# Convolution input projection by Strassen's seven products, on normed input, with the second layer's memory keys computed first

## The chip, the cores and the metric

One core of a Trainium2 chip runs the whole program. The metric is device time in microseconds, the median of several executions; the profile is of one execution. Five engines work from queues of their own: TensorE (PE; its weight loads are listed as PEld), VectorE (DVE), ScalarE (ACT), GpSimd (POOL) and SyncE (SP), which here issues the transfers between DRAM and the on-chip memory SBUF. TensorE writes its sums into PSUM, from which VectorE and ScalarE read. All data are float32.

## The reference

1024 tokens of 1024 features pass two layers. Layer 0 has windowed attention and retention side by side. Layer 1 is a gated convolution over the tokens. After each comes a cross-attention with four heads into 256 memory tokens, and at the end a norm. What the change touches is layer 1's convolution, and the keys of the cross-attention behind it:

```python
def conv_mixer(xn, w_in, conv_w, conv_b, w_out):
    s = xn.shape[1]
    gb, gc, u, gate = jnp.split(xn @ w_in, 4, axis=-1)
    z = gc * u
    zp = jnp.pad(z, ((0, 0), (C_CONV - 1, 0), (0, 0)))
    conv = conv_b
    for j in range(C_CONV):
        conv = conv + zp[:, j:j + s] * conv_w[j]
    y = gb * conv * jax.nn.silu(gate)
    return y @ w_out
```

Here `xn = rmsnorm(x, g)`: x times the gain g of its feature and times R, the inverse root of the token's mean square. `w_in` is 1024 x 4096. The keys are `memn @ wkv[:, :1024]`, 1024 features for 256 memory tokens.

## The kernel before

**Layout.** Activations lie with features on the 128 partitions and tokens along the row: eight tiles of 128 x 1024. A weight tile is 128 x 1024 too: for one output tile of 128 features, the eight 128 x 128 blocks of the contraction side by side.

**Precision.** A float32 number is split into a part `hi`, rounded to the type float32r, and the rest `lo`. A product takes three matmuls, hi hi + hi lo + lo hi (`mm3`, L125 to L130). ScalarE copies `hi`, VectorE subtracts to get `lo`: L64 and L65 for weights, L144 and L145 (`split`) for most others, L156 and L157 where a gain is applied on the way.

**Weights.** `Weights` streams weight tiles in a fixed order: a raw tile is loaded (L53, two buffers `wraw`), split into `whi` and `wlo` (three buffers each), and taken by a projection. When tile i is taken, tiles up to i + 2 are prepared.

**A projection.** `dense` (L132) computes 128 output features: for each half of the tokens, eight contraction tiles by three matmuls of 512 columns, 24 matmuls into one PSUM bank; then a function evacuates it.

**The convolution stage.** `out_proj` of layer 0's cross-attention adds the residual (L227), and squares and sums the features (L186, L188, L202). `gained` splits x times the gain of its feature (L156, L157). `norm` makes R from the sums, by two matmuls for each half of the tokens (L195, L196) and a chain on ScalarE and VectorE (L167 to L172). R isn't in the matmuls' input: evacuation multiplies by it (`scaled`, L214). `conv_in` (L478) takes eight groups of four weight tiles (gate, gb, gc, u), 32 calls of `dense`:

```python
            for done in (gate, gb, gc, u):
                self.dense(xs, done)
            if m < 5:
                next(kv)
```

`gate` and `gc` are scaled at evacuation and once more by R on GpSimd (L488, L495), since the other factor lacks its R; `gb` and `u` multiply PSUM by that (L491, L498). Three taps and the product with y1 follow (L504 to L509).

**The memory keys.** `mem_k` computes one tile of 128 key features at each step: 24 matmuls of 256 columns. Five steps stand behind the first five groups, three behind the last (`for _ in kv: pass`); then the convolution's outputs are split and projected by `out_proj`, with the memory values (`mem_v`) in between. The normed memory is kept in DRAM and loaded as four tiles `mn`.

**The order.** Buffers are named by tag, and each tag has a fixed number (L108: `xh`, `xl`, `r` 8 each, `T` and `t` 5, `e` and `v` 4); an instruction that writes a buffer waits until the readers of what was in it are done. A planner orders each engine's instructions ahead of time, by a simulated time line: earlier instructions of the program go first, but whatever its simulation finds ready may go in between. On the chip each engine follows that fixed order and waits by semaphores.

## Time and profile before

| | us |
|---|---|
| median of 3 runs (1514.28 to 1515.32) | 1514.37 |
| span of the profiled execution, first to last instruction | 1513.2 |
| TensorE busy in it | 1483.5 |
| VectorE, ScalarE, GpSimd busy | 769.1, 564.8, 230.3 |
| convolution projection: first evacuation of y to last of z | 799.3 to 1149.2 |
| layer 1's three last key tiles | 1148 to 1157 |

The profiled execution has no time of its own beside its span; the median of the runs is 1.2 us above it. In the profile's rows, `x16 | 11.0, 690` means 16 instructions, 11.0 us busy in all, 690 ns each on average. A row of a time line gives the start in us, the length in us, engine, source line, operation, output and inputs, shape, and the count where equal neighbours are merged; in brackets the idle time before it and what ended that. A row of one tile gives the shortest, median and longest instruction in ns, then the first and last start in us. Matmuls overlap, so their busy lengths are not to be added up.

### The profile page before, as it was taken

Reading aid. Unit: us, or ns where it says so; the run is one execution under the profiler, and the core shown is the slowest. Engines: PE = TensorE matmul, PEld = TensorE weight load, DVE = VectorE, ACT = ScalarE, POOL = GpSimd, SP = SyncE. Lnnn points to the kernel's source line nnn. Section 1 sums busy time; section 2 is a strip of 40 time slices with the busy share of each in tenths; the row PEclk is TensorE's granted clock in tenths of the full one; section 3 lists DMA queues with packets and bytes.
Section 4 is the critical chain, followed back from the end, with each engine's and each line's share of the span. In section 5 each row is a group of like instructions: output and inputs, shape, how many; then the busy total and the mean of one; then the engine's idle time right before and its main releaser. Section 6 shows DMA issues by size and latency. Waiting matters only on the chain.

```text
span 1513.2 us, 18550 instructions
## 1 busy us (share of the span) xinstructions
PE 1483.5 (98%) x7410; PEld 1256.1 (83%) x7410; DVE 769.1 (51%) x1143; ACT 564.8 (37%) x983; POOL 230.3 (15%) x157
## 2 busy tenths in 40 slices
PE   8999999999999999999999999999999999999996
PEld 6878888888788888888888888888888888888996
DVE  7656765556673356444354333332336336446555
ACT  6434652433463244343243111211115225334554
POOL 2300103233401210000211111111110120000233
PEclk9999999999999999999999999999999999999998
DMA  5410104121464521002522221111123532111464
GB/s 212 165 44 29 56 29 139 58 82 43 139 209 153 167 82 44 29 29 70 193 81 102 63 63 56 56 56 56 42 84 113 180 127 74 36 30 40 133 206 151
DMA packets 44421, 140.77 MB, mean 93 GB/s; under 512 B 5552, under 2 KB 11824, under 8 KB 44080
## 3 DMA queue, kind: packets, MB, share of 16 engines
q1 hardware_dynamic: 44336, 139.60, 28.3%
q8 instruction: 58, 0.95, 0.3%
q14 instruction: 27, 0.22, 0.0%
HBM read 112.32 MB, written 23.07 MB: 89 GB/s over the span
## 4 chain that ended last, share of the span: by engine, by line
PE 85%; DVE 5%; DMA 4%; POOL 2%; ACT 1%; issue 1%; SPq 1%; DVEq 0%; POOLq 0%; ACTq 0%
PE psd L130 23%; PE psd L128 23%; PE psd L129 23%; PE pssc L130 3%; PE pssc L129 3%; PE pssc L128 3%; PE psa L128 2%; PE psa L129 2%; PE psa L130 2%; PE psa L311 1%; DMA swap<-bk 1%; DMA swap<-bq 1%; PE psa L621 1%; POOL bk L346 1%; POOL bq L346 1%
## 5 line engine op out<-in xcount | busy, mean ns | idle before, releaser
L128 PE MATMUL psd<-xh,whi 128*128 128x512 f32 (+2 forms) x1736 | 662.0, 384 | 8.4 <-ACT whi L64 7.3
L129 PE MATMUL psd<-xl,whi 128*128 128x512 f32 (+2 forms) x1736 | 663.9, 383 | 0.0
L130 PE MATMUL psd<-xh,wlo 128*128 128x512 f32 (+2 forms) x1736 | 663.1, 383 | 0.0
L128 PEld LDWEIGHTS psd<-xh,whi 128*128 128x128 f32 x1736 | 326.2, 188 | 69.5 <-ACT whi L64 7.8
L129 PEld LDWEIGHTS psd<-xl,whi 128*128 128x128 f32 x1736 | 326.3, 188 | 59.5 <-DVE xl L157 0.3
L130 PEld LDWEIGHTS psd<-xh,wlo 128*128 128x128 f32 x1736 | 326.2, 188 | 59.5
L64 ACT CAST whi<-wraw 128x1024 fp32r<-128x1024 f32 (+1 forms) x155 | 162.0, 1046 | 428.1 <-PE psd L129 306.7
L65 DVE TENSOR_TENSOR wlo<-wraw,whi 128x1024 fp32r<-128x1024 f32 (+1 forms) x155 | 200.6, 1295 | 68.0 <-ACT whi L64 66.1
L188 POOL TENSOR_TENSOR ssq<-ssq,xold 128x512 f32<-128x512 f32 (+2 forms) x54 | 78.1, 1446 | 573.6 <-ACT xold L186 484.3
L227 DVE TENSOR_TENSOR xnew<-psd,xold 128x512 f32<-128x512 f32 x48 | 32.9, 690 | 147.2 <-PE psd L130 143.8
L186 ACT ACTIVATE xold<-xnew 128x512 f32<-128x512 f32 (+2 forms) x63 | 36.4, 580 | 89.2 <-DVE xnew L227 48.9
L144 ACT CAST Th<-psa 128x512 fp32r<-128x512 f32 (+1 forms) x62 | 34.2, 588 | 68.9 <-PE psa L311 36.8
L145 DVE TENSOR_TENSOR Tl<-psa,Th 128x512 fp32r<-128x512 f32 (+1 forms) x62 | 42.1, 686 | 28.3 <-ACT Th L144 28.3
L488 POOL TENSOR_TENSOR y<-y,R 128x512 f32<-128x512 f32 x16 | 24.2, 1514 | 185.4 <-ACT y L487 185.4
L214 DVE TENSOR_TENSOR q<-psd,R 128x512 f32<-128x512 f32 x32 | 22.1, 691 | 53.9 <-PE psd L130 53.8
L611 ACT ACTIVATE P<-pssc,mx 128x256 f32<-128x256 f32 x64 | 29.5, 473 | 43.2 <-DVE mx L609 43.2
L214 DVE TENSOR_TENSOR z<-psd,R 128x512 f32<-128x512 f32 x16 | 11.1, 692 | 61.5 <-PE psd L130 61.5
L495 POOL TENSOR_TENSOR z<-z,R 128x512 f32<-128x512 f32 x16 | 20.7, 1295 | 132.6 <-DVE z L214 132.6
L491 DVE TENSOR_TENSOR y<-psd,y 128x512 f32<-128x512 f32 x16 | 11.0, 690 | 56.9 <-PE psd L130 56.9
L128 PE MATMUL psd<-mn,whi 128*128 128x256 f32 x128 | 36.8, 290 | 2.9 <-DVE K L145 2.9
L130 PE MATMUL psd<-mn,wlo 128*128 128x256 f32 x128 | 37.1, 290 | 0.8 <-DVE wlo L65 0.8
L498 DVE TENSOR_TENSOR z<-psd,z 128x512 f32<-128x512 f32 x16 | 11.1, 691 | 52.2 <-PE psd L130 52.2
(234 smaller groups left out, 1875.5 us busy)
## 6 DMA issues: line engine op xcount, KB each, us to landing
wraw<-w_o SPq DMA_DIRECT2D x32, 512.0 KB, 3.8
wraw<-w_o_in SPq DMA_DIRECT2D x32, 512.0 KB, 3.6
wraw<-w_e_in SPq DMA_DIRECT2D x25, 512.0 KB, 3.7
xold<-x SPq DMA_DIRECT2D x24, 512.0 KB, 4.7
x<-xnew SPq DMA_DIRECT2D x24, 512.0 KB, 2.6
wraw<-w_k SPq DMA_DIRECT2D x16, 512.0 KB, 3.8
wraw<-w_v SPq DMA_DIRECT2D x16, 512.0 KB, 3.6
wraw<-w_q SPq DMA_DIRECT2D x16, 512.0 KB, 3.6
```

The costliest lines, as they stand in the source:

```text
L64: self.nc.scalar.copy(hi[:, c], raw[:, c])
L65: self.nc.vector.tensor_tensor(lo[:, c], raw[:, c], hi[:, c].bitcast(F32), op=ALU.subtract)
L128: mm(o, ah, bh, start=first, stop=False)
L129: mm(o, ah, bl, start=False, stop=False)
L130: mm(o, al, bh, start=False, stop=last)
L144: self.nc.scalar.copy(hi, src)
L145: (eng or self.nc.vector).tensor_tensor(lo, src, hi.bitcast(F32), op=ALU.subtract)
L186: nc.scalar.activation(sq, x, AF.Square)
L188: eng.tensor_tensor(self.ssq[:, a:b], self.ssq[:, a:b], sq, op=ALU.add)
L214: return lambda a, b, ps: self.nc.vector.tensor_tensor(out(a, b), ps, self.R[:, a:b], op=ALU.mult)
L227: nc.vector.tensor_tensor(new[:, a:b], ps, old[:, a:b], op=ALU.add)
L346: nc.gpsimd.tensor_tensor(t, t, cos, op=ALU.mult)
```

## The change

**Strassen.** Two feature tiles (gate with gb, gc with u) are computed together. Their weights are a 2 x 2 block matrix A: two output tiles by two halves of the contraction (four blocks each). The normed input is a 2 x 2 block matrix B: halves of the contraction by halves of the tokens. Winograd's form needs seven block products where the plain form needs eight. Each is four contraction tiles by three matmuls of 512 columns, 12 matmuls. Four of the seven are added up in PSUM on a bank that already holds a product; ScalarE copies three intermediate sums to SBUF (`kept`), VectorE adds them at evacuation.

**Factors of the weights.** `factor` loads both raw tiles of a pair, forms S1 to S4 on GpSimd, and splits each of seven factors (128 x 512) into one page that holds `hi` and `lo`. `whi` and `wlo` buffers, three each, serve as six pages. A raw pair occupies both `wraw` buffers until its last factor is split.

**Factors of the input.** `right_factors` multiplies x by gain and R in place, on VectorE, forms T1 to T4 on GpSimd (T1, T3 and T4 in place of B11, B12 and B21), and splits the seven factors, in buffers of the tags `xh`, `xl`, `e`, `T` and `n`. R and the sums of squares are buffers of the new tag `n` now, and are allocated anew behind the convolution.

**Keys.** `keys_out` computes layer 1's eight key tiles in one block ahead of the convolution and stores them to DRAM; `keys_in` loads them behind it. The normed memory is loaded twice.

The other hunks take comments away. The core of the diff:

```diff
@@ -38,41 +38,97 @@
 class Weights:
-    def __init__(self, tc, pool, order):
-        self.nc, self.pool, self.order = tc.nc, pool, order
+    FACTORS = ("A11", "A12", "S2", "S1", "S3", "S4", "A22")
+    def __init__(self, tc, pool, sums, order):
+        self.nc, self.pool, self.sums, self.order = tc.nc, pool, sums, order
         self.raw, self.parts = {}, {}
+        self.units = []
+        for i, entry in enumerate(order):
+            if isinstance(entry, tuple):
+                self.units += [(i, f) for f in self.FACTORS]
+            else:
+                self.units.append((i, None))
+        self.tags = []
+        pages = 0
+        for _, f in self.units:
+            self.tags.append(("whi", "wlo") if f is None else (("whi", "wlo")[pages % 2],))
+            pages += f is not None
         self.next = 0
         self.used = 0
+        self.factors = {}
     def load(self, i):
-        if i < len(self.order) and i not in self.raw:
-            t = self.pool.tile([P, D], F32, tag="wraw", bufs=WRAW, name=f"wraw{i}")
+        if i >= len(self.order) or i in self.raw:
+            return
+        entry = self.order[i]
+        tiles = []
+        for k, ap in enumerate(entry if isinstance(entry, tuple) else (entry,)):
+            t = self.pool.tile([P, D], F32, tag="wraw", bufs=WRAW, name=f"wraw{i}_{k}")
             for c in halves(i == 0):
-                self.nc.sync.dma_start(t[:, c], self.order[i][:, c])
-            self.raw[i] = t
-    def prepare(self, upto):
-        while self.next <= min(upto, len(self.order) - 1):
-            i = self.next
+                self.nc.sync.dma_start(t[:, c], ap[:, c])
+            tiles.append(t)
+        self.raw[i] = tiles
+    def page(self, tag, name):
+        return self.pool.tile([P, D], F32R, tag=tag, bufs=WHI if tag == "whi" else WLO, name=name)
+    def whole(self, u, i):
+        raw = self.raw.pop(i)[0]
+        hi, lo = self.page("whi", f"whi{u}"), self.page("wlo", f"wlo{u}")
+        for c in halves(i == 0):
+            self.nc.scalar.copy(hi[:, c], raw[:, c])
+            self.nc.vector.tensor_tensor(lo[:, c], raw[:, c], hi[:, c].bitcast(F32),
+                                         op=ALU.subtract)
+        self.parts[u] = (hi, lo)
+    def factor(self, u, i, f):
+        if f == self.FACTORS[0]:
+            a, b = self.raw[i]
+            s13, s24 = self.sums(), self.sums()
+            F = {"A11": a[:, :H], "A12": a[:, H:], "A21": b[:, :H], "A22": b[:, H:],
+                 "S1": s13[:, 0, :], "S3": s13[:, 1, :], "S2": s24[:, 0, :], "S4": s24[:, 1, :]}
+            tt = self.nc.gpsimd.tensor_tensor
+            tt(F["S1"], F["A21"], F["A22"], op=ALU.add)
+            tt(F["S2"], F["S1"], F["A11"], op=ALU.subtract)
+            tt(F["S3"], F["A11"], F["A21"], op=ALU.subtract)
+            tt(F["S4"], F["A12"], F["S2"], op=ALU.subtract)
+            self.factors = F
+        t = self.page(self.tags[u][0], f"wf{u}")
+        src, hi, lo = self.factors[f], t[:, :H], t[:, H:]
+        self.nc.scalar.copy(hi, src)
+        self.nc.vector.tensor_tensor(lo, src, hi.bitcast(F32), op=ALU.subtract)
+        self.parts[u] = (hi, lo)
+        if f == self.FACTORS[-1]:
+            self.raw.pop(i)
+    def prepare(self, upto=None):
+        while self.next < len(self.units) and (upto is None or self.next <= upto):
+            u = self.next
+            live = [t for v in range(self.used, u + 1) for t in self.tags[v]]
+            if live.count("whi") > WHI or live.count("wlo") > WLO:
+                return
+            i, f = self.units[u]
             self.load(i)
-            raw = self.raw.pop(i)
-            hi = self.pool.tile([P, D], F32R, tag="whi", bufs=WHI, name=f"whi{i}")
-            lo = self.pool.tile([P, D], F32R, tag="wlo", bufs=WLO, name=f"wlo{i}")
-            for c in halves(i == 0):
-                self.nc.scalar.copy(hi[:, c], raw[:, c])
-                self.nc.vector.tensor_tensor(lo[:, c], raw[:, c], hi[:, c].bitcast(F32),
-                                             op=ALU.subtract)
-            self.parts[i] = (hi, lo)
+            if f is None:
+                self.whole(u, i)
+            else:
+                self.factor(u, i, f)
             self.next += 1
-            self.load(i + 1)
+            if self.next < len(self.units) and self.units[self.next][0] != i:
+                self.load(i + 1)
     def take(self):
-        i = self.used
+        u = self.used
+        self.prepare()
         self.used += 1
-        self.prepare(i + WHI - 1)
-        return self.parts.pop(i)
+        return self.parts.pop(u)
...
-        self.w = Weights(tc, self.wp, order)
+        self.w = Weights(tc, self.wp, lambda: self.buf("T", "ws", (P, 2, H)), order)
...
@@ -121,16 +179,17 @@
         return self.pp.tile([P, H], F32, tag=tag, bufs={"d": 3, "sc": 2, "a": 3}[tag],
                             name=f"ps{tag}_{self.count}")
-    def mm3(self, o, ah, al, bh, bl, first, last):
+    def mm3(self, o, ah, al, bh, bl, first, last, more=False):
         mm = self.nc.tensor.matmul
-        mm(o, ah, bh, start=first, stop=False)
-        mm(o, ah, bl, start=False, stop=False)
-        mm(o, al, bh, start=False, stop=last)
+        mm(o, ah, bh, start=first, stop=False, skip_group_check=more)
+        mm(o, ah, bl, start=False, stop=False, skip_group_check=more)
+        mm(o, al, bh, start=False, stop=last, skip_group_check=more)
     def dense(self, xs, done, parts=((0, H), (H, S)), tags="d"):
         wh, wl = self.w.take()
...
+    def right_factors(self, x, gain):
+        nc = self.nc
+        half = (slice(0, H), slice(H, S))
+        B = {f"B{i + 1}{j + 1}": [x[4 * i + k][:, half[j]] for k in range(4)]
+             for i in range(2) for j in range(2)}
+        for f in ("B11", "B21", "B22", "B12"):
+            for k in range(4):
+                g = 8 * gain + 4 * (f[1] == "2") + k
+                h = half[f[2] == "2"]
+                nc.vector.scalar_tensor_tensor(B[f][k], B[f][k], self.gains[:, g : g + 1],
+                                               self.R[:, h], ALU.mult, ALU.mult)
+        out = {}
+        def split(f, src):
+            two = [None, None]
+            for k in range(4):
+                if f in ("B22", "T3"):
+                    if k % 2 == 0:
+                        two = self.buf("e", f, (P, 4, H), F32R)
+                    hi, lo = two[:, 2 * (k % 2), :], two[:, 2 * (k % 2) + 1, :]
+                else:
+                    tag = "xh" if k % 2 else "xl"
+                    if f == "T4":
+                        tag = "T" if k < 2 else "n"
+                    t = self.buf(tag, f, dt=F32R)
+                    hi, lo = t[:, :H], t[:, H:]
+                self.split(hi, lo, src[k])
+                out.setdefault(f, []).append((hi, lo))
+        tt, sub = nc.gpsimd.tensor_tensor, ALU.subtract
+        split("B11", B["B11"])
+        T1, T3, T4 = B["B11"], B["B12"], B["B21"]
+        T2 = [self.buf("t", "T2", (P, H)) for _ in range(4)]
+        for k in range(4):
+            tt(T1[k], B["B12"][k], B["B11"][k], op=sub)
+            tt(T2[k], B["B22"][k], T1[k], op=sub)
+        split("B21", B["B21"])
+        split("T2", T2)
+        split("T1", T1)
+        for k in range(4):
+            tt(T3[k], B["B22"][k], B["B12"][k], op=sub)
+        split("T3", T3)
+        split("B22", B["B22"])
+        for k in range(4):
+            tt(T4[k], B["B21"][k], T2[k], op=sub)
+        split("T4", T4)
+        return out
+    def strassen(self, B, out):
+        def product(ps, f, first):
+            ah, al = self.w.take()
+            for k, (bh, bl) in enumerate(B[f]):
+                c = slice(k * P, k * P + P)
+                self.mm3(ps, ah[:, c], al[:, c], bh, bl, first and k == 0, k == 3, not first)
+        def kept(ps):
+            t = self.buf("t", "kept", (P, H))
+            self.nc.scalar.copy(t, ps)
+            return t
+        a, b, c = self.ps("sc"), self.ps("d"), self.ps("a")
+        product(a, "B11", True)
+        p1 = kept(a)
+        product(b, "B21", True)
+        out(0, 0, b, p1)
+        product(a, "T2", False)
+        u2 = kept(a)
+        product(c, "T1", True)
+        p5 = kept(c)
+        product(a, "T3", False)
+        out(1, 1, a, p5)
+        product(c, "B22", False)
+        out(0, 1, c, u2)
+        product(a, "T4", False)
+        out(1, 0, a, None)
+    def times(self, B, d, act=None):
+        nc = self.nc
+        half = (slice(0, H), slice(H, S))
+        kept = []
+        def out(i, j, ps, more):
+            c = d[:, half[j]]
+            if i == 0:
+                nc.vector.tensor_tensor(c, ps, more, op=ALU.add)
+                if act is not None:
+                    nc.scalar.activation(c, c, act)
+                if j:
+                    nc.gpsimd.tensor_tensor(c, c, kept[0], op=ALU.mult)
+            elif j:
+                t = self.buf("t", "second", (P, H))
+                nc.vector.tensor_tensor(t, ps, more, op=ALU.add)
+                kept.append(t)
+            else:
+                nc.vector.tensor_tensor(c, ps, c, op=ALU.mult)
+        self.strassen(B, out)
+    def conv_in(self, B):
         nc = self.nc
         ys = []
         for m in range(KT):
             w = [self.convw[:, 8 * j + m : 8 * j + m + 1] for j in range(4)]
             y1, z, cv = self.buf("v", "y1"), self.buf("v", "z"), self.buf("r", "cv")
-            def gate(a, b, ps):
-                self.scaled(lambda a, b: y1[:, a:b])(a, b, ps)
-                nc.scalar.activation(y1[:, a:b], y1[:, a:b], AF.Silu)
-                nc.gpsimd.tensor_tensor(y1[:, a:b], y1[:, a:b], self.R[:, a:b], op=ALU.mult)
-            def gb(a, b, ps):
-                nc.vector.tensor_tensor(y1[:, a:b], ps, y1[:, a:b], op=ALU.mult)
-            def gc(a, b, ps):
-                self.scaled(lambda a, b: z[:, a:b])(a, b, ps)
-                nc.gpsimd.tensor_tensor(z[:, a:b], z[:, a:b], self.R[:, a:b], op=ALU.mult)
-            def u(a, b, ps):
-                nc.vector.tensor_tensor(z[:, a:b], ps, z[:, a:b], op=ALU.mult)
-            for done in (gate, gb, gc, u):
-                self.dense(xs, done)
-            if m < 5:
-                next(kv)
+            self.times(B, y1, AF.Silu)
+            self.times(B, z)
             nc.scalar.activation(cv, z, AF.Identity, bias=w[3], scale=w[2])
             nc.vector.scalar_tensor_tensor(cv[:, 1:], z[:, : S - 1], w[1], cv[:, 1:],
                                            ALU.mult, ALU.add)
...
+    def keys_out(self, mem):
+        nc = self.nc
+        self.kd = self.dp.tile([2, P, KT, M], F32, name="kd")
+        for m in range(KT):
+            wh, wl = self.w.take()
+            ps = self.ps("d")[:, :M]
+            for kt in range(KT):
+                c = slice(kt * P, kt * P + P)
+                self.mm3(ps, wh[:, c], wl[:, c], mem[0][kt], mem[1][kt], kt == 0, kt == KT - 1)
+            hi, lo = (self.buf("k", "K", (P, M), F32R) for _ in range(2))
+            self.split(hi, lo, ps)
+            nc.sync.dma_start(self.kd[0, :, m, :], hi.bitcast(F32))
+            nc.sync.dma_start(self.kd[1, :, m, :], lo.bitcast(F32))
+    def keys_in(self):
+        K = [self.buf("e", "K", (P, KT, M), F32R) for _ in range(2)]
+        for i in range(2):
+            self.nc.sync.dma_start(K[i].bitcast(F32), self.kd[i])
+        return K
...
@@ -691,14 +856,12 @@
         self.norm(rest)
         ys = self.cross(xs, K, V)
         x, rest = self.out_proj(ys, xd[0], xd[1])
-        xs = self.gained(x, 3)
         self.norm(rest)
+        self.keys_out(self.mem_parts(1, "T"))
+        ys = self.conv_in(self.right_factors(x, 3))
+        self.new_norm()
         mem = self.mem_parts(1, "T")
-        kv = self.mem_k(mem)
-        K = next(kv)
-        ys = self.conv_in(xs, kv)
-        for _ in kv:
-            pass
+        K = self.keys_in()
         kv = self.mem_v(mem)
         V = next(kv)
         ys = [self.split_k(y) for y in ys]
...
     o_in, k1 = tiles("w_o_in"), tiles("w_k1")
     order = (tiles("w_e_in", "w_k0") + mixed("w_e_out", 1, "w_v0", 2) + tiles("w_q0", "w_o0")
-             + [t for m in range(KT) for t in o_in[4 * m : 4 * m + 4] + (k1[m : m + 1] if m < 5 else [])]
-             + k1[5:] + mixed("w_o_out", 1, "w_v1", 2) + tiles("w_q1", *["w_o1"] * len(LAST)))
+             + k1 + list(zip(o_in[::2], o_in[1::2])) + mixed("w_o_out", 1, "w_v1", 2) + tiles("w_q1", *["w_o1"] * len(LAST)))
```

More of the change, by code (lines that the diff above doesn't have):

```diff
@@ L103, in __init__ @@
         nc.vector.tensor_scalar(self.mean_vr, self.mean_d, float(D // P), None, ALU.mult)
-        self.R = self.cp.tile([P, S], F32, name="R")
-        self.ssq = self.cp.tile([P, S], F32, name="ssq")
-    BUFS = {"xh": 8, "xl": 8, "r": 8, "e": 4, "T": 5, "v": 4, "t": 5, "k": 4}
+        self.new_norm()
+    BUFS = {"xh": 8, "xl": 8, "r": 8, "e": 4, "T": 5, "v": 4, "t": 5, "k": 4, "n": 2}
     def buf(self, tag, name, shape=(P, S), dt=F32):
@@ L113, in buf, with new_norm @@
                             name=f"{name}_{self.count}")
+    def new_norm(self):
+        self.R, self.ssq = self.buf("n", "R"), self.buf("n", "ssq")
     def small(self, name):
@@ L460, in even_layer @@
             v = self.to_tokens(v, "bv")
-            self.w.prepare(self.w.used + WHI - 1)
+            self.w.prepare()
             if h == 3:
@@ L639, in cross @@
                 self.dense(xs, self.scaled(lambda a, b: q[dt][:, a:b]))
[L640 removed]
+            self.w.prepare()
             if head < 3:
@@ L709, in run @@
         self.last_proj(ys, xd[2], LAST)
-        assert self.w.used == len(self.w.order)
+        assert self.w.used == len(self.w.units)
 def _tiles(w):
```

3 lines of the change are left out of this document (1 added, 2 removed).

## The prediction

> **What bounds the kernel now.** I read the page's busy shares and its chain first, then the busy time by engine for the stages around the change, then single instructions.
>
> ```profile
> PE 1483.5 (98%) x7410; PEld 1256.1 (83%) x7410; DVE 769.1 (51%) x1143; ACT 564.8 (37%) x983; POOL 230.3 (15%) x157
> ...
> PE 85%; DVE 5%; DMA 4%; POOL 2%; ACT 1%; issue 1%; SPq 1%; DVEq 0%; POOLq 0%; ACTq 0%
> ...
> 784.80:807.00 22.20, 21.98 (x97) 17.85 (x96) 14.51 (x19) 15.46 (x19) 1.29 (x1) 1.00 0.48 166
> 807.00:1148.00 341.00, 340.87 (x1560) 284.63 (x1561) 124.89 (x128) 59.82 (x68) 43.65 (x31) 1.00 0.19 58
> 1148.00:1157.00 9.00, 8.80 (x72) 8.56 (x71) 9.00 (x10) 7.33 (x9) 0.00 (x0) 1.00 0.17 49
> 1157.00:1190.00 33.00, 33.00 (x149) 27.36 (x148) 15.48 (x17) 11.36 (x14) 3.09 (x2) 1.00 0.58 196
> ```
>
> The last four rows are the entry of the convolution projection, its body, the three memory-key tiles behind it, and the output projection (columns: stretch, its length, busy PE, PEld, DVE, ACT, POOL, clock, DMA). TensorE is busy throughout: 340.87 of 341.00 us in the body, at full clock. A matmul taken away there is worth its whole interval, as long as the other engines keep up. VectorE (124.89) and GpSimd (43.65) have much room, on average; the entry is where that must be looked at.
>
> A matmul's 0.39 us is no price, since they overlap. The interval between starts is:
>
> ```profile
> 1143.63 0.39 PE L129 MATMUL psd<-xl,whi 128*128 128x512 f32 x1
> ...
> 1146.81 0.39 PE L128 MATMUL psd<-xh,whi 128*128 128x512 f32 x1
> ...
> 1150.08 0.28 PE L129 MATMUL psd<-mn,whi 128*128 128x256 f32 x1
> ...
> 1150.92 0.28 PE L130 MATMUL psd<-mn,wlo 128*128 128x256 f32 x1
> ```
>
> The first two rows are 14 intervals apart: 0.227 us for 512 columns. The last two are 7 apart: 0.120 us for the keys' 256 columns.
>
> **Removed: matmuls.** A pair of feature tiles took 2 x 2 x 24 = 96 matmuls; seven products of 12 take 84. Over 16 pairs 192 go: 192 x 0.227 = **-43.5 us**. One product lasts 12 x 0.227 = 2.72 us, one pair 19.1.
>
> **Added at the entry: normed factors before the first products.** Before, raw inputs were split, matmuls began at once, and the norms R were needed only at evacuation. Now everything hangs behind R: 16 multiplications by gain and R (VectorE), 16 sums T1 to T4 (GpSimd), 28 splits (ScalarE copy, VectorE subtraction). The eight key tiles stand in front as cover: 192 x 0.120 = 23.0 us of TensorE. Prices:
>
> ```profile
> 784.77 0.68 DVE L227 TENSOR_TENSOR xnew<-psd,xold 128x512 f32<-128x512 f32 x1
> 785.37 2.47 DVE L157 SCALAR_TENSOR_TENSOR xl<-xnew,gains,xh 128x1024 fp32r<-128x1024 f32 x2
> ...
> 1149.84 3.48 DVE L145 TENSOR_TENSOR xl<-cv,xh 128x1024 fp32r<-128x1024 f32 x3
> ...
> 1156.71 0.74 DVE L145 TENSOR_TENSOR K<-psd,K 128x256 fp32r<-128x256 f32 x2
> ```
>
> Back to back, a 512-wide VectorE operation takes 0.60 (785.37 - 784.77), a 1024-wide one 1.16 (3.48 / 3), a key split 0.37. Until the first pair's last product can run, VectorE must do, from 784.8:
>
> - 16 normings, 28 splits, 7 weight factors, 3 evacuations: 54 x 0.60 = 32.4
> - 5 key weight tiles not yet split: 5.8; 8 key splits: 3.0
> - the last evacuation, and what is left of R (some eight operations): 5.4
>
> That is 46.6 us. GpSimd does 16 sums T and the pair's 4 weight sums S, 20 operations. Whether the two run side by side decides this term:
>
> ```profile
> 819.12 1.29 POOL L495 TENSOR_TENSOR z<-z,R 128x512 f32<-128x512 f32 x1 [4.15 <-DVE z L214]
> ...
> 819.21 2.29 DVE L65 TENSOR_TENSOR wlo<-wraw,whi 128x1024 fp32r<-128x1024 f32 x1 [0.17 <-ACT whi L64]
> ...
> 830.09 1.23 DVE L65 TENSOR_TENSOR wlo<-wraw,whi 128x1024 fp32r<-128x1024 f32 x1
> ...
> 1449.64 1.23 DVE L65 TENSOR_TENSOR wlo<-wraw,whi 128x1024 fp32r<-128x1024 f32 x1
> 1450.78 5.59 DVE L257 TENSOR_TENSOR xnew<-xnew,R 128x384 f32<-128x384 f32 x5
> ...
> 1449.74 4.59 POOL L257 TENSOR_TENSOR xnew<-xnew,R 128x384 f32<-128x384 f32 x3 [10.51 <-DVE R L172]
> ...
> L214 DVE TENSOR_TENSOR z<-psd,R x16: 691/692/692, 812.9 to 1137.5; 128x512 f32<-128x512 f32 x16
> ```
>
> The same VectorE subtraction takes 1.23 alone and 2.29 beside a GpSimd operation of 1.29: 1.06 us lost. At the kernel's end 384-wide multiplications of both engines take 1.12 and 1.53 each, while a 512-wide one on VectorE alone takes 0.68. An operation with one input in PSUM (last row) does not stretch. So two-input SBUF work of VectorE and GpSimd goes one after the other: 20 x 1.06 = 21.2 more, less 3.3 for evacuations and key splits, which read PSUM. 46.6 + 21.2 - 3.3 + 0.7 (the last three matmuls) = 65.2 us, against 23.0 + 19.1 + 0.9 (four matmuls for R) = 43.0 of TensorE work: **+22.2 us** of stall. Lower end: no lock, 46.6 + 0.7 - 43.0 = 4.3. Upper end: 1.29 for each, nothing beside PSUM reads, 3 us idle until R: 46.6 + 25.8 + 0.7 + 3 - 43.0 = 33.1. I take the middle one, by the row of 2.29.
>
> The Trainium skill, page "SBUF — State Buffer", section "Who interferes with whom", says that a VectorE instruction with two SBUF inputs and a GpSimd instruction that reads SBUF exclude each other for the whole instruction. The rows agree in kind, at 1.06 of 1.29; by the rule's whole instruction this stall would be 20 x 0.23 = 4.6 longer.
>
> **A slow clock after the stall.**
>
> ```profile
> 438.00:446.00 8.00, 6.10 (x35) 5.88 (x36) 7.23 (x11) 5.79 (x10) 0.00 (x0) 0.79 0.59 189
> ...
> 439.34 0.36 PE L128 MATMUL psd<-mn,whi 128*128 128x256 f32 x1 [2.92 <-DVE K L145]
> ```
>
> After an idle time of 2.92 us the clock granted in these 8 us was 0.79: 8 x 0.21 = **+1.7 us**, once, when the last wait is over. Between 0 (stalls cut into pieces under 1 us) and 3.4 (twice). While TensorE waits anyway, a slow clock costs nothing.
>
> The Trainium skill, page "TensorE: Matmul & The Clock Gate", section "What's actually happening", lets the clock fall to half only after an idle window of about 3.4 us. The row shows it fall after 2.92 us. By the rule, stalls in pieces shorter than 3.4 us would cost nothing here, and the sum would be 1497.9.
>
> **The body.**
>
> ```profile
> L144 ACT CAST Th<-psa 128x512 fp32r<-128x512 f32 (+1 forms) x62 | 34.2, 588 | 68.9 <-PE psa L311 36.8
> ...
> wraw<-w_o_in SPq DMA_DIRECT2D x32, 512.0 KB, 3.6
> ...
> 1142.50 0.39 PE L130 MATMUL psd<-xh,wlo 128*128 128x512 f32 x1
> ...
> 1143.00 0.69 DVE L498 TENSOR_TENSOR z<-psd,z 128x512 f32<-128x512 f32 x1 [2.37 <-PE psd L130]
> ```
>
> For two pairs (38.1 us of TensorE): VectorE 14 weight factors and 8 evacuations at 0.60, and the convolution's three operations, about 3.6: 16.8. GpSimd 8 sums and 2 multiplications, 10 x 1.06 = 10.6 if all collide. 27.4 of 38.1: no engine becomes the bound. Six single pages hold factors, so each is split up to five products (13.6 us) ahead. Both raw tiles of a pair are free only after the last factor (A22) is split, 2.7 + 1.3 us into the pair; then loads of 3.6 us, and 4 sums of 1.29: S2 is there near 11, wanted at 24.5. The weight loads keep their cover; without it each pair would wait their 3.6.
>
> Tighter is the reuse of PSUM: four products are added onto a bank that must first be read. Three wait for a copy by ScalarE (0.59), with one product, 2.72, in between. The fourth, the pair's last, waits for a VectorE evacuation, which starts 0.3 us after its product's last interval (1143.00 - 1142.50 - 0.227) and so has 2.72 - 0.3 - 0.69 = 1.7 us to spare; one collision (1.06) ahead of it is hidden, two (2.12) cost 0.4. With two in every second pair: 16 x 0.2 = **+3.3 us**. Behind it on VectorE stand the next factors, with pages to spare. Ends: 0, and 1.6 a pair (below).
>
> Norm multiplications by R leave (32 of GpSimd, nothing waited); key stores add 16 small issues on SP ahead of weight loads, within the VectorE-bound stretch.
>
> **The exit.** The three key tiles (72 x 0.120 = 8.6 us) that covered the last convolution tile's tail are gone.
>
> ```profile
> L498 DVE TENSOR_TENSOR z<-psd,z x16: 682/692/692, 823.9 to 1149.2; 128x512 f32<-128x512 f32 x16
> L504 ACT ACTIVATE cv<-z,convw x8: 1240/1242/1248, 830.0 to 1151.2; 128x1024 f32<-128x1024 f32 x8
> L505 DVE SCALAR_TENSOR_TENSOR cv<-z,convw,cv x8: 1275/1284/1285, 831.3 to 1154.4; 128x1023 f32<-128x1023 f32 x8
> L507 DVE SCALAR_TENSOR_TENSOR cv<-z,convw,cv x8: 1270/1284/1285, 832.6 to 1157.4; 128x1022 f32<-128x1022 f32 x8
> L509 DVE TENSOR_TENSOR cv<-cv,y x8: 1211/1216/1227, 835.3 to 1160.7; 128x1024 f32<-128x1024 f32 x8
> L144 ACT CAST xh<-cv x8: 1042/1052/1055, 1143.6 to 1161.9; 128x1024 fp32r<-128x1024 f32 x8
> L145 DVE TENSOR_TENSOR xl<-cv,xh x8: 1214/1218/1225, 1144.7 to 1163.0; 128x1024 fp32r<-128x1024 f32 x8
> ```
>
> From the last product to the eighth split: 0.69 + 1.24 + 1.28 + 1.28 + 1.22 + 1.05 + 1.22 = 8.0 us bare; before, with other work between, 15.0 (1149.2 to 1164.2). The output projection can use seven split tiles meanwhile: 42 x 0.227 = 9.5, since the factors' buffers come free from the last pair's first product on. So 0 to 5.5; I take **+1.5**, nearer the bare chain. The keys' reload (2 MB) is wanted only after the output projection; it costs nothing.
>
> **Sum.** -43.5 + 22.2 + 1.7 + 3.3 + 1.5 = -14.8. Span 1513.2 - 14.8 = 1498.4; the runs' median 1514.37 is 1.2 above the span, so 1499.6.
>
> **Rivals.**
> - *The port does not bind at the entry*: the planner finds an order in which sums fall beside PSUM reads and gaps. Stall 4.3, exit 1.5, no more: 1514.4 - 43.5 + 5.8 = 1476.7. For it: VectorE is half idle over the span. Against: the 2.29 row.
> - *The gain is eaten*: every cost at its upper end but the body's, 33.1 + 1.7 + 3.3 + 5.5 = 43.6, gives 1514.5, no change. For it: queues in order, one sum after one split, R late.
> - *Slower*: in each pair the last product waits for the evacuation ahead of it, because VectorE's queue holds a weight factor (0.69) behind a sum (1.29), and a convolution operation (1.28) in front: 3.3 - 1.7 = 1.6 us, 16 times 25.6 instead of 3.3: 1521.9. It makes the kernel slower from 1.1 us a pair on ((14.8 + 3.3) / 16). Against it: 27.4 of 38.1 us.
>
> **Chances.** The forecast 0.50 (its own range 1492 to 1510), the free port 0.20, the gain eaten 0.13, slower 0.17. A difference of 0.2% (3 us) is the least this kernel's measurement can tell. The forecast and the free port lie below it, and 0.05 of the eaten gain: faster 0.75, same 0.08, slower 0.17. The range reaches down to the free port and up into the slower case: 1476 to 1517.
>
> **What will show it.** Right: a stretch of some 65 us behind the second output projection, VectorE full, GpSimd operations above 1.29, about 22 us of idle TensorE, and a low clock; then an unbroken body, 16 pairs of 19.1 us. Wrong: VectorE idle there while TensorE waits (a buffer or R would be the cause), VectorE splits at 0.60 beside sums, or gaps in every pair before the last product.

## The result and the profile after

The changed kernel takes **1505.99 us** (median of 4 runs, 1504.75 to 1510.04), the kernel before beside it 1514.84 (4 runs, 1514.28 to 1518.75). The ratio is 0.9939, with a 95% interval of 0.9919 to 0.9958: 0.6% faster. The forecast was 1499.6 with a range of 1476 to 1517. The sign and the range held; of the forecast 14.8 us, some 9 came.

The profiled execution of the changed kernel was the slowest of its four (1510.04 us, span 1508.2). It was already 1.9 us behind when the last evacuation of the second output projection started, in a part of the program that the change leaves alone; the rows do not say why. So the stages are compared by their own lengths. First the page of the kernel after:

```profile
PE 1450.5 (96%) x7218; PEld 1226.8 (81%) x7218; DVE 878.7 (58%) x1259; ACT 626.1 (42%) x1129; POOL 349.1 (23%) x221
...
PE   8999999999999999999997599999999999999996
```

The 192 matmuls are gone (7410 to 7218). Where TensorE was busy throughout in the kernel before, a hole has come into two slices. The same row of the page before:

```profile
PE   8999999999999999999999999999999999999996
```

Next a time line of the kernel after, with rows of several engines (SPq are transfers issued on SyncE). Its first and last row are the last evacuations of the second and the third output projection, the stage around the change; between them stands the entry.

```profile
786.69 0.69 DVE L286 TENSOR_TENSOR xnew<-psd,xold 128x512 f32<-128x512 f32 x1 [1.86 <-PE psd L189]
...
788.83 0.33 SPq L74 DMA_DIRECT2D wraw<-w_k  x1
789.26 1.99 SPq L693 DMA_DIRECT2D mn<-memn  x4
790.40 0.51 PE L254 MATMUL psa<-sq,mean_dr 128*128 128x512 f32 x1 [3.30 <-ACT sq L203]
795.44 1.01 PE L187 MATMUL psd<-mn,whi 128*128 128x256 f32 x3 [3.44 <-DMA mn<-memn]
...
806.13 0.68 DVE L231 TENSOR_TENSOR R<-rt,rs 128x512 f32<-128x512 f32 x1
...
831.57 0.39 PE L189 MATMUL psd<-B,wf 128*128 128x512 f32 x1
...
838.17 1.71 POOL L97 TENSOR_TENSOR ws<-wraw 128x512 f32<-128x512 f32 x1
838.68 6.76 DVE L204 TENSOR_TENSOR B<-xnew,B 128x512 fp32r<-128x512 f32 x4
840.58 0.80 PE L187 MATMUL psa<-T,wf 128*128 128x512 f32 x1 [8.62 <-ACT wf L104]
849.92 0.68 DVE L105 TENSOR_TENSOR wf<-ws,wf 128x512 fp32r<-128x512 f32 x1
850.52 2.48 DVE L204 TENSOR_TENSOR T<-xnew,T 128x512 fp32r<-128x512 f32 x4
850.65 0.80 PE L189 MATMUL psa<-T,wf 128*128 128x512 f32 x1 [8.85 <-DVE wf L105]
...
854.73 0.68 DVE L105 TENSOR_TENSOR wf<-ws,wf 128x512 fp32r<-128x512 f32 x1
855.08 0.63 PE L187 MATMUL pssc<-T,wf 128*128 128x512 f32 x1
...
1261.58 0.68 DVE L286 TENSOR_TENSOR xnew<-psd,xold 128x512 f32<-128x512 f32 x1
```

The same end of the stage in the kernel before, whose start, 784.77, the prediction shows:

```profile
1266.94 0.68 DVE L227 TENSOR_TENSOR xnew<-psd,xold 128x512 f32<-128x512 f32 x1
```

Before: 1266.94 - 784.77 = 482.2 us. After: 1261.58 - 786.69 = 474.9. The stage is 7.3 us shorter, where the matmuls alone give 43.5, so **36.2 us** were given back. The busy time by engine for stretches of the kernel after says where (columns as in the prediction):

```profile
787.00:860.00 73.00, 44.32 (x251) 38.49 (x251) 65.70 (x77) 36.48 (x64) 37.66 (x22) 0.79 0.38 123
...
791.00:802.00 11.00, 7.09 (x31) 6.29 (x32) 10.93 (x19) 6.19 (x11) 0.00 (x0) 0.53 0.55 216
...
840.00:856.00 16.00, 6.57 (x15) 4.73 (x16) 16.00 (x19) 7.20 (x12) 8.16 (x5) 0.50 0.13 36
...
872.00:1137.00 265.00, 265.00 (x1171) 219.49 (x1170) 178.69 (x178) 98.55 (x164) 119.06 (x70) 1.00 0.19 58
1137.00:1193.00 56.00, 56.00 (x249) 46.39 (x248) 30.64 (x31) 22.46 (x26) 5.86 (x5) 1.00 0.68 225
```

It is the entry alone. TensorE works in 44.32 of its 73 us: 28.7 us are idle. The kernel before had 72.65 us of work in the same 73:

```profile
787.00:860.00 73.00, 72.65 (x332) 60.32 (x331) 33.52 (x38) 22.79 (x27) 8.26 (x6) 1.00 0.27 90
```

In two stretches of the kernel after the clock is at about half: 7.09 us of work at 0.53 and 6.57 at 0.50 hold 7.09 x 0.47 + 6.57 x 0.50 = 6.6 us more. Together 35.3 of the 36.2. Body and exit have no idle time at all.

Three things are to be seen in the rows of the entry above. The key tiles start only at 795.44: their memory tiles are issued at 789.26, behind a weight load that waits for its raw buffer, and land 6 us later. Two products, on B11 and B21, are done at 831.8. Then TensorE wants the product of S1 and T1. Its weight sum (L97) starts at 838.17, behind 14 sums T on GpSimd; ScalarE copies its `hi` part, and VectorE subtracts at 849.92, behind four splits of B22 and five other operations. That is the 8.62 and the 8.85. VectorE's last split of T4 ends at 853.0, and its split of the pair's last weight factor at 855.4 (854.73 + 0.68). Only three of the seven products are done by then; the fourth has just begun (855.08).

### The profile page after: what moved, and what is told of

Its sections match the earlier page's. It is cut to its first block, busy times and chain, and to the rows that moved or that the text cites. A ratio compares the mean times of both kernels' runs of the same rounds, so it can differ in the third digit from the quotient of the medians.

```text
span 1508.2 us, 18628 instructions
## 1 busy us (share of the span) xinstructions
PE 1450.5 (96%) x7218; PEld 1226.8 (81%) x7218; DVE 878.7 (58%) x1259; ACT 626.1 (42%) x1129; POOL 349.1 (23%) x221
## 5 line engine op out<-in xcount | busy, mean ns | idle before, releaser
L187 PE MATMUL psd<-xh,whi 128*128 128x512 f32 (+2 forms) x1224 | 464.1, 382 | 7.4 <-ACT whi L85 6.7
L188 PE MATMUL psd<-xl,whi 128*128 128x512 f32 (+2 forms) x1224 | 465.6, 381 | 0.0
L189 PE MATMUL psd<-xh,wlo 128*128 128x512 f32 (+2 forms) x1224 | 464.7, 381 | 0.0
L187 PEld LDWEIGHTS psd<-xh,whi 128*128 128x128 f32 x1224 | 230.4, 188 | 48.4 <-ACT whi L85 7.3
L189 PEld LDWEIGHTS psd<-xh,wlo 128*128 128x128 f32 x1224 | 230.7, 188 | 39.9 <-DVE wlo L86 0.2
L188 PEld LDWEIGHTS psd<-xl,whi 128*128 128x128 f32 x1224 | 230.8, 189 | 39.7
L86 DVE TENSOR_TENSOR wlo<-wraw,whi 128x1024 fp32r<-128x1024 f32 (+1 forms) x123 | 155.5, 1266 | 60.0 <-ACT whi L85 59.8
L245 ACT ACTIVATE xold<-xnew 128x512 f32<-128x512 f32 (+2 forms) x63 | 36.4, 580 | 94.6 <-DVE xnew L286 49.4
L187 PE MATMUL pssc<-T,wf 128*128 128x512 f32 x192 | 74.9, 390 | 0.0
L188 PE MATMUL pssc<-T,wf 128*128 128x512 f32 x192 | 74.9, 390 | 0.0
L189 PE MATMUL pssc<-T,wf 128*128 128x512 f32 x192 | 74.7, 389 | 0.0
L105 DVE TENSOR_TENSOR wf<-wraw,wf 128x512 fp32r<-128x512 f32 x48 | 67.1, 1400 | 9.7 <-ACT wf L104 9.5
L105 DVE TENSOR_TENSOR wf<-ws,wf 128x512 fp32r<-128x512 f32 x64 | 48.1, 754 | 12.1 <-ACT wf L104 12.1
```

Source lines behind the costliest of these rows:

```text
L86: self.nc.vector.tensor_tensor(lo[:, c], raw[:, c], hi[:, c].bitcast(F32), op=ALU.subtract)
L105: self.nc.vector.tensor_tensor(lo, src, hi.bitcast(F32), op=ALU.subtract)
L187: mm(o, ah, bh, start=first, stop=False, skip_group_check=more)
L188: mm(o, ah, bl, start=False, stop=False, skip_group_check=more)
L189: mm(o, al, bh, start=False, stop=last, skip_group_check=more)
L245: nc.scalar.activation(sq, x, AF.Square)
```

## The experiments

The kernel before had a median between 1515.0 and 1516.4 beside them. Stage means the time between the two last evacuations above.

**The keys alone.** The plain convolution of before, with the keys computed first and kept in DRAM (`keys_out` and `keys_in` as in the change):

```diff
-        kv = self.mem_k(mem)
-        K = next(kv)
-        ys = self.conv_in(xs, kv)
-        for _ in kv:
-            pass
+        self.keys_out(mem)
+        ys = self.conv_in(xs)
+        K = self.keys_in()
...
-             + [t for m in range(KT) for t in o_in[4 * m : 4 * m + 4] + (k1[m : m + 1] if m < 5 else [])]
-             + k1[5:] + mixed("w_o_out", 1, "w_v1", 2) + ...
+             + k1 + o_in + mixed("w_o_out", 1, "w_v1", 2) + ...
```

> The plain convolution of before, with only the keys moved: eight key tiles first, stored to DRAM and loaded again. Theory A (the block of keys costs nothing by itself; it only stands where the factors are late): the plain matmuls need no norm and can fill what the keys leave open, 1514 to 1518 us against 1514.8 before. Rival B (the move itself costs the gain: late memory tiles, a stretch of 256-column matmuls with two weight engines busy, the lost cover at the exit): 1522 to 1530.

Measured: 1531.37, ratio 1.0104 (1.0089 to 1.0119). This part alone costs 16 us, still 1.4 above the rival's range. The second kernel loads the memory tiles ahead of the norm:

```diff
+        mem = self.mem_parts(1, "T")
         self.norm(rest)
-        mem = self.mem_parts(1, "T")
```

> The plain convolution with the keys first (1531 us), and the four loads of the normed memory ahead of the norm. Theory A (the block of keys costs 16 us because its memory tiles land some 13 us after TensorE is free, and the clock falls meanwhile): 1515 to 1518 us. Rival B (the norm's matmuls, which stand ahead of the keys and wait for the last evacuation, hold TensorE; or the keys' own rate does): 1524 to 1531.

Measured: 1517.87, ratio 1.0018 (1.0008 to 1.0028), as the theory had it. The stretch behind the output projection, keys alone (columns as above):

```profile
784.00:800.00 16.00, 4.86 (x12) 2.42 (x12) 14.04 (x18) 11.50 (x15) 0.00 (x0) 0.70 0.46 169
```

And the same stretch with the early loads:

```profile
784.00:800.00 16.00, 14.40 (x97) 13.03 (x96) 15.05 (x17) 14.33 (x19) 0.00 (x0) 1.00 0.27 82
```

4.86 us of work in 16 become 14.40, and the clock goes from 0.70 to 1.00. The place of four loads is worth 13.5 us here: TensorE stands still in front of the keys.

**The same loads in the changed kernel.** `mem = self.mem_parts(1, "T")` is moved ahead of `self.norm(rest)`, as above.

> The changed kernel with the four loads of the normed memory written ahead of the norm instead of behind it. Theory A (the keys start 8 us late because the memory tiles land at 795.4, and that late start holds the second half's R by way of a weight split ahead of it on VectorE): 6 to 8 us less, 1498 to 1500 us against 1506. Rival B (the entry is as long as VectorE's work, whenever the keys start): 1504 to 1507.

Measured: 1507.8, ratio 0.9952 (0.9937 to 0.9967): no gain over the change's 0.9939, and 0.8 us above the rival's range. The time line of this kernel:

```profile
783.34 0.69 DVE L286 TENSOR_TENSOR xnew<-psd,xold 128x512 f32<-128x512 f32 x1 [1.86 <-PE psd L189]
...
801.36 0.58 PE L187 MATMUL psd<-mn,whi 128*128 128x256 f32 x1 [2.75 <-DVE K L204]
806.30 0.68 DVE L231 TENSOR_TENSOR R<-rt,rs 128x512 f32<-128x512 f32 x1
...
852.66 0.80 PE L188 MATMUL pssc<-T,wf 128*128 128x512 f32 x1 [10.51 <-DVE T L204]
```

The keys now run at once, with 2.75 us as their longest wait. But R's second half (L231) comes 23.0 us behind the last evacuation (806.30 - 783.34), in the change 19.4 (806.13 - 786.69), and the idle time has moved behind the keys. Late loads were in the way, but what stood behind them decided.

**The keys behind the convolution**, so that nothing covers the entry:

```diff
-        self.keys_out(self.mem_parts(1, "T"))
         ys = self.conv_in(self.right_factors(x, 3))
         self.new_norm()
         mem = self.mem_parts(1, "T")
+        self.keys_out(mem)
...
-             + k1 + list(zip(o_in[::2], o_in[1::2])) + ...
+             + list(zip(o_in[::2], o_in[1::2])) + k1 + ...
```

> The changed kernel with the eight key tiles behind the convolution instead of ahead of it: the entry has no cover. Theory A (the keys fill 23 us of a stretch that VectorE and GpSimd bound; without them these two save 9 us of key work): 23 - 9 = 14 us more, 1518 to 1522 us. Rival B (the block costs as much as it covers, as with the plain convolution, where it cost 16 us): 1503 to 1508.

Measured: 1520.93, ratio 1.0036 (1.0023 to 1.005), 14.9 us over the change. The keys in front do cover the entry: about 15 of their 23.0 us, net of the work that they bring to VectorE, and without them the change is slower than before.

**Who makes the sums.** Four kernels. In the first, the 16 sums T go to VectorE; in the second, the first pair's four sums S; in the third, both; in the fourth, the 16 sums T are left out: T1 to T4 are blocks of the input as they stand.

```diff
-        tt, sub = nc.gpsimd.tensor_tensor, ALU.subtract
+        tt, sub = nc.vector.tensor_tensor, ALU.subtract
```

> The changed kernel with the 16 sums T on VectorE instead of GpSimd. Theory A (VectorE and GpSimd work in series on two-input SBUF operations): 16 x 0.60 replaces 16 x 1.06, 7.4 us less in series, and the weight sums S no longer stand behind 14 sums T on GpSimd, up to 10 us more: 1489 to 1499 us against 1506. Rival B (VectorE's own work is the bound, GpSimd beside it costs nothing): 16 x 0.60 = 9.6 us more, 1514 to 1517.

```diff
-            tt = self.nc.gpsimd.tensor_tensor
+            tt = (self.nc.gpsimd if any(self.units[v][1] for v in range(u)) else self.nc.vector).tensor_tensor
```

> The changed kernel with the first pair's four weight sums S on VectorE; the other pairs as before. Theory A (product S1 x T1 and all behind it wait for S1, whose sum stands behind 14 sums T on GpSimd, and whose split stands behind nine others on VectorE): the idle time of 17.5 us before that product falls to 5 to 10, 1494 to 1500 us against 1506. Rival B (the products wait for VectorE's whole work, in whatever order): four sums more on VectorE, four fewer on GpSimd, 1505 to 1508.

> The changed kernel with the 16 sums T and the first pair's four sums S on VectorE: GpSimd has nothing in the entry. Theory A (the two engines shut each other out: with T on VectorE alone, the first sum S on GpSimd took 9.41 us instead of 1.29, and the products waited for it): that wait goes, VectorE works at 0.60 throughout, 8 to 11 us less than T alone (1504), 1493 to 1497 us. Rival B (what counts is the fixed order of VectorE's queue, which puts the split of S2 late in any case): 1501 to 1505.

```diff
         for k in range(4):
-            tt(T1[k], B["B12"][k], B["B11"][k], op=sub)
-            tt(T2[k], B["B22"][k], T1[k], op=sub)
+            pass
...
-        split("T2", T2)
+        split("T2", B["B22"])
...
-            tt(T3[k], B["B22"][k], B["B12"][k], op=sub)
+            pass
...
-            tt(T4[k], B["B21"][k], T2[k], op=sub)
+            pass
```

> The changed kernel without the 16 sums T (the untouched blocks are split and multiplied in their place, so four of the seven products have other factors than they should; the rest of the work is all there). Theory A (the sums on GpSimd lengthen the entry by what they shut VectorE out, 16 x 1.06 = 17 us, and by the delay of S1): 14 to 20 us less, 1486 to 1492 us against 1506. Rival B (VectorE's 46.6 us bound the entry whether GpSimd works or not, and the fixed order does the rest): 1500 to 1506.

| | us | ratio to before |
|---|---|---|
| the change | 1505.99 | 0.9939 (0.9919 to 0.9958) |
| sums T on VectorE | 1504.47 | 0.9935 (0.9919 to 0.9952) |
| first sums S on VectorE | 1502.49 | 0.9915 (0.9900 to 0.9929) |
| both | 1498.62 | 0.9892 (0.9877 to 0.9906) |
| no sums T at all | 1493.07 | 0.9855 (0.9838 to 0.9871) |

Each of the four times falls between the range of its theory and that of its rival, so each edit did some of what was expected of it. Without the sums T 12.9 us go. That is what they cost beside VectorE's own work, both by holding VectorE up and by delaying S1; this kernel does not part the two. With the sums T on VectorE its operations are back at 0.60 us, but the sums S, left on GpSimd, come to a standstill:

```profile
824.86 9.41 POOL L97 TENSOR_TENSOR ws<-wraw 128x512 f32<-128x512 f32 x1 [48.58 <-DMA wraw<-w_o_in]
...
827.05 2.48 DVE L204 TENSOR_TENSOR T<-xnew,T 128x512 fp32r<-128x512 f32 x4
...
834.97 0.80 PE L187 MATMUL psa<-T,wf 128*128 128x512 f32 x1 [7.17 <-ACT wf L104]
```

One sum takes 9.41 us, and TensorE waits 7.17 for its ScalarE copy.

The kernel with only the first sums S on VectorE shows what the order is worth:

```profile
783.83 0.69 DVE L286 TENSOR_TENSOR xnew<-psd,xold 128x512 f32<-128x512 f32 x1 [1.86 <-PE psd L189]
...
849.50 0.67 DVE L204 TENSOR_TENSOR T<-xnew,T 128x512 fp32r<-128x512 f32 x1
...
1252.14 0.68 DVE L286 TENSOR_TENSOR xnew<-psd,xold 128x512 f32<-128x512 f32 x1
```

VectorE's last split of T4 ends 850.2 - 783.8 = 66.3 us behind the last evacuation, as in the change (853.0 - 786.7). But four products of the first pair are done by then, and not two and a part of the third, and the stage takes 468.3 us instead of 474.9.

With both on VectorE, the long sum is gone from GpSimd, though TensorE still has one wait of 7.37 us, now for a split in VectorE's own queue. The time line of this kernel:

```profile
783.76 0.69 DVE L286 TENSOR_TENSOR xnew<-psd,xold 128x512 f32<-128x512 f32 x1 [1.86 <-PE psd L189]
...
839.95 0.67 DVE L105 TENSOR_TENSOR wf<-ws,wf 128x512 fp32r<-128x512 f32 x1
840.55 1.88 DVE L204 TENSOR_TENSOR T<-xnew,T 128x512 fp32r<-128x512 f32 x3
840.67 0.80 PE L189 MATMUL psa<-T,wf 128*128 128x512 f32 x1 [7.37 <-DVE wf L105]
...
844.76 0.67 DVE L105 TENSOR_TENSOR wf<-ws,wf 128x512 fp32r<-128x512 f32 x1
...
1251.67 0.68 DVE L286 TENSOR_TENSOR xnew<-psd,xold 128x512 f32<-128x512 f32 x1
```

The last split of T4 ends 842.4 - 783.8 = 58.7 us behind the last evacuation, against 853.0 - 786.7 = 66.3 in the change: 7.6 us less, and the kernel is 7.4 us faster. Up to the split of the pair's last weight factor it is 61.7 us (845.4 - 783.8) against 68.7.

**Both, and the early loads.** The three edits together:

> T and the first pair's S on VectorE, and the loads of the normed memory ahead of the norm. Theory A (the keys' late start, some 8.5 us idle and 3 us of slow clock, is a loss of its own now that GpSimd is out of the entry): 8 to 11 us less than T and S alone, 1488 to 1491 us against 1498.6. Rival B (as with the early loads alone, what the keys gain is lost again, since VectorE's work ends no sooner): 1496 to 1500.

Measured: 1498.45, ratio 0.9885 (0.9870 to 0.9900): the same as without the early loads, as the rival had it. Again the keys run at once, and VectorE's work sets what comes behind.

**Splitting late.** In the kernel with both sums on VectorE, each input factor is split, in the program's order, only ahead of the first product that takes it:

```diff
-        split("B11", B["B11"])
...
+        class Late(dict):
+            def __missing__(_, f):
+                if f == "T2":
+                    for k in range(4):
+                        tt(T1[k], B["B12"][k], B["B11"][k], op=sub)
+                        tt(T2[k], B["B22"][k], T1[k], op=sub)
+                if f == "T1":
+                    for k in range(4):
+                        tt(T3[k], B["B22"][k], B["B12"][k], op=sub)
+                        tt(T4[k], B["B21"][k], T2[k], op=sub)
+                split(f, {"T1": T1, "T2": T2, "T3": T3, "T4": T4}.get(f) or B[f])
+                return out[f]
```

> The sums T and the first pair's sums S are on VectorE, as in t_s_vector (1498.62), and each factor of the input is split in the program only just ahead of the first product that takes it, where before all 28 splits stood ahead of all products. VectorE's work until the last split of T4 is the same, some 58 us. Theory A (what counts is how many products are still to do when VectorE has done its series: in t_s_vector the third product's second half came only behind nine other operations of VectorE, and five products of 2.72 us stood behind it): two to three products move ahead of the end of the series, so 5 to 8 us less, 1490 to 1494, and TensorE's longest idle time in the entry, 7.37 us, falls below 4. Rival B (the planner already puts on VectorE what its simulation finds ready, whatever the order of the program, and the pages for the factors come free only behind the keys): 1497 to 1500, with an idle time above 6 us before the third product.

Measured: 1498.87, ratio 0.9883 (0.9866 to 0.9899). The theory has the idle time right and the gain wrong. The time line and three stretches of it:

```profile
784.83 0.69 DVE L286 TENSOR_TENSOR xnew<-psd,xold 128x512 f32<-128x512 f32 x1 [1.86 <-PE psd L189]
...
832.13 0.49 PE L187 MATMUL psa<-T,wf 128*128 128x512 f32 x1 [2.29 <-ACT T L203]
834.73 0.80 PE L187 MATMUL pssc<-T,wf 128*128 128x512 f32 x1 [2.11 <-ACT wf L104]
838.18 0.80 PE L188 MATMUL psa<-T,wf 128*128 128x512 f32 x1 [2.22 <-DVE T L204]
...
845.26 1.30 DVE L204 TENSOR_TENSOR T<-xnew,T 128x512 fp32r<-128x512 f32 x2
...
1249.85 0.68 DVE L286 TENSOR_TENSOR xnew<-psd,xold 128x512 f32<-128x512 f32 x1
```

```profile
828.00:833.00 5.00, 2.34 (x10) 1.38 (x8) 5.00 (x10) 3.98 (x8) 0.00 (x0) 1.00 0.08 26
833.00:838.00 5.00, 1.23 (x2) 0.58 (x2) 5.00 (x9) 4.97 (x9) 0.00 (x0) 0.59 0.00 0
838.00:844.00 6.00, 5.06 (x11) 3.57 (x12) 6.00 (x11) 2.97 (x6) 0.00 (x0) 0.50 0.32 93
```

No idle time is above 2.29 behind the keys, where there was one of 7.37. But VectorE's series is the same work, and ends 61.7 us behind the last evacuation (845.26 + 1.30 - 784.83), as it did with both sums on VectorE, and 36 matmuls of the pair are still to come then (47 there). And pauses of 2.1 to 2.3 us in a row bring the clock down as one long pause did: it is full up to 833 and half soon after, in the second of them, and 5.06 us of work in 838 to 844 run at 0.50. In the profiled executions the stage is 2.9 us shorter (465.0 for 467.9). In the runs' times no gain can be told, since the medians agree and the two intervals overlap; the two profiled spans agree too (1497.0 and 1496.8), because the parts ahead of and behind the stage, whose program is the same, came out 3.1 us longer. The runs do not show why.

**More cover.** Layer 1's memory values, like the keys, are computed ahead of the convolution and kept in DRAM; first with both sums on VectorE, then with the early loads too:

```diff
-        self.keys_out(self.mem_parts(1, "T"))
+        mem = self.mem_parts(1, "T")
+        self.keys_out(mem)
+        self.values_out(mem)
         ys = self.conv_in(self.right_factors(x, 3))
...
+        K, V = self.keys_in(), self.values_in()
...
-             + k1 + list(zip(o_in[::2], o_in[1::2])) + mixed("w_o_out", 1, "w_v1", 2) + ...
+             + k1 + tiles("w_v1") + list(zip(o_in[::2], o_in[1::2])) + tiles("w_o_out") + ...
```

> As T and S on VectorE, and layer 1's memory values (96 matmuls of 512 columns, 21.8 us of TensorE) are computed behind the keys too, stored to DRAM and loaded again, so that they stand in the entry instead of between the tiles of the output projection. Theory A (the entry is bound by VectorE, and TensorE work that needs no input factor fills it): 21.8 us more cover against 11.7 us more VectorE work (8 weight tiles, 4 splits), 8 to 10 us less than T and S alone, 1484 to 1489 us if that comes to 1494. Rival B (the values lengthen the entry as much as they fill it): the same as T and S alone, or 2 to 5 us more.

> As the run before, with layer 1's values in the entry too. Theory A (with the memory tiles in time, VectorE's queue is no longer held by weight splits that wait for TensorE, and the 21.8 us of cover count): 4 to 10 us less than without the values, 1480 to 1487 us. Rival B (the values' 11.7 us of VectorE work take what their cover gives): within 3 us of the run without them.

Measured: 1499.17, ratio 0.9895 (0.9880 to 0.9910), no gain; then **1494.47**, ratio 0.9863 (0.9840 to 0.9887), 4.0 us under the kernel with the three edits. That is the low edge of the theory's 4 to 10, and far from its 1480 to 1487, which counted on a gain from the early loads; the two intervals overlap. The entry of the last one:

```profile
787.00:860.00 73.00, 59.83 (x313) 50.85 (x311) 65.33 (x100) 37.70 (x62) 0.00 (x0) 0.91 0.51 151
```

TensorE is busy for 59.83 of 73 us instead of 44.32, VectorE for 65.33, as in the change. The values bring their own splits and evacuations to VectorE, the engine that is full. With 1.4% under the kernel before, this has the lowest median of the kernels that compute all; its interval overlaps that of the one with both sums on VectorE (0.9892) as well, so whether it beats it, and by how much, is left open.

## Why the prediction was right, and where it was not

- **Matmuls, -43.5.** Right: 7410 to 7218, and from y's first last-product evacuation at 871.8 to z's last at 1155.5, fifteen pairs take 283.7 us, 18.9 each where 19.1 was forecast (two of the second pair's products had already run, and some matmuls of the output projection ran among the last).
- **The entry: mechanism right.** VectorE and GpSimd do exclude each other. Beside each other, each has one operation per 1.7 us: GpSimd 1.71 (838.17) where 1.29 is its length alone, VectorE 6.76 / 4 = 1.69 (838.68) where it is 0.60 once GpSimd rests (2.48 / 4 at 850.52). The series was forecast to be 64.5 us of work without a gap. VectorE worked 64.9 of the 68.7 us up to the split of the pair's last weight factor and stood idle for 3.8. (Two of the three evacuations counted came later, and six key weight tiles instead of five were left to split, which cancels.) The rival of the free port is ruled out by these rows and by the 12.9 us that went with the sums T. The Trainium skill, page "SBUF — State Buffer", section "Who interferes with whom", calls it a lock held for the whole instruction; a pair of 1.29 and 0.60 would then take 1.89, and the rows show 1.7, nearer the 1.06 + 0.60 of the forecast.
- **The entry: the failed step** is the sentence that the series counts until "the first pair's last product can run", with 0.7 us for the last three matmuls behind it. It takes all other work of TensorE, 43.0 us with the keys and the whole pair, to be done by then but for three matmuls. When VectorE's series was over, at 855.4, 47 of the pair's 84 matmuls had not begun, 10.7 us. So the price of the entry is the series and what is left behind it, less 43.0. The idle time (28.7 us, not 22.2) and the slow clock are how TensorE spends that price. Five kernels bear this out, within 0.7 us in four of them:

| | series, us | matmuls not begun at its end | series + these x 0.227 - 43.0 | given back: 43.5 less what the stage gained |
|---|---|---|---|---|
| the change | 68.7 | 47 | 36.4 | 36.2 |
| sums T on VectorE | 62.5 | 51 | 31.1 | 32.9 |
| first sums S on VectorE | 66.3 | 31 | 30.3 | 29.6 |
| both | 61.7 | 47 | 29.4 | 29.2 |
| both, splitting late | 61.7 | 36 | 26.9 | 26.3 |

The series ends with the last split of T4 or of the pair's weight factors, whichever is later. In the second kernel the first eight or so matmuls behind the series were still 0.43 us apart instead of 0.227, which is most of the 1.8 us that are missing. The account was made from the traces; no run was made to test it alone.

- **Cover taken as ready.** The key tiles were counted from the first moment; their four loads, moved with them, were given no cost. They came 8 us late. Alone this is 13.5 us (the two kernels with keys and plain convolution). In the changed kernel taking it away gained nothing, since the series stood behind it: it was a wrong step that did not decide the time.
- **Slow clock, +1.7, at most 3.4.** Too small: 6.6 us. The forecast took one slow stretch at the end of one wait. There were two, in the first key tiles and in the third product, with TensorE work in both. The forecast's row at 439.34, in the kernel before, was also read a little short: the clock was still full when the matmuls began again there, and fell at about 440.4, after a second pause of 0.56 us.
- **Body, +3.3: nothing.** 265.00 of 265.00 us busy at full clock. VectorE 178.69 and GpSimd 119.06 add up to more than the stretch, since the time in which one is held by the other counts as its own; no product waited for it. **Exit, +1.5: nothing**: 56.00 of 56.00.
- **Sum.** Forecast: -43.5 + 23.9 + 3.3 + 1.5 = -14.8. The stage: -43.5 + 28.7 + 6.6 and 0.9 that no row accounts for, = -7.3. The entry was 12.3 us dearer, body and exit 4.8 cheaper. Of the 12.3, 4.2 are the longer series (68.7 for 64.5) and 10.0 the matmuls left behind it (10.7 for 0.7); the 1.7 forecast for the slow clock lie within these.
- **The rivals.** "The gain is eaten" had the entry's cost about right, 33.1 + 1.7 for 36.2, but put 8.8 more into body and exit. "Slower" did not happen: there is no gap in any pair.

**Left open.** In the kernel with the late splits, 8.6 of the 26.3 us given back are not idle time (17.7). The half clock takes 7.0 of them (TensorE's busy time times the missing clock, added up in steps of 0.5 us), about as much as the 7.4 with both sums on VectorE and the 6.4 that the same count gives for the change; 1.6 stay without an account. R's second half comes 17 to 23 us behind the last evacuation in every kernel with seven products, in VectorE's fixed order; moving it alone was not tried.

## What to carry to other kernels

Work that stands in front of a pipeline as its cover has to be ready itself: its loads' place in the issue queue is part of its price, and it must not use the engine it is to cover. A stall behind a long series isn't its length less all other work, but less the work that can run before it ends; ask which products wait for the first, the middle and the last of it. Where VectorE and GpSimd both read two SBUF operands, sharing the work between them did not pay in this kernel: giving the sums to VectorE alone took 7.4 us off.

## What the runs showed of the hardware

- **GpSimd can be held for many VectorE operations.** The 9.41 us of one sum, alone 1.29, cover fourteen VectorE operations of 0.60 each, one behind the other, in the kernel with the sums T on VectorE; the sum ends 1.1 us after VectorE pauses (833.1). In the change, from 824.7 on, with sums waiting on GpSimd all the time, the two took turns, at 1.7 us a pair. What decides between the one and the other was not found.
- **The clock comes down to half without one long pause.** In the kernel with the late splits a pause of 2.29 us, one matmul of 0.49 and the larger part of a pause of 2.11 were enough: the clock was full up to 833, half from 834 on, and full again only at 844.2. The Trainium skill, page "TensorE: Matmul & The Clock Gate", section "What's actually happening", has half clock after an idle window of about 3.4 us; the 0.50 agrees, but no single idle time there reached 2.4 us. Cutting one wait into pieces saved idle time there (17.7 us for 20.5 with both sums on VectorE), but hardly any half clock (7.0 for 7.4).
- **Stretched operations in the body cost nothing.** In the changed kernel's body a convolution tap takes longer than before (the groups of tile z, shortest, median and longest in ns; 1284 was the median before):

```profile
L649 DVE SCALAR_TENSOR_TENSOR cv<-z,convw,cv x8: 1285/2309/2323, 893.9 to 1157.6; 128x1023 f32<-128x1023 f32 x8
```

1.02 us longer, as the lock would have it, and TensorE was busy throughout.
